# Two value projections as one Strassen product, the first heads' queries and keys as another, and the forget gates computed apart

## The chip, the cores and the metric

The kernel runs on one core of a Trainium2 chip, as one program. The metric is the device time of that core in microseconds (us); less is better. In the text PE is the matrix engine (TensorE), DVE the vector engine (VectorE), ACT the scalar engine (ScalarE), POOL GpSimd, SP the engine that issues the DMAs. PEld is the loading of a stationary operand (the weights of a matmul) into the matrix engine; it runs beside matmuls.

## The reference, cut to what matters

One layer of a hybrid encoder on x, 1024 tokens of 1024 channels, float32. All branches start from one projection of x; these are its parts that the change touches.

```python
proj = x @ w_in
q_a, k_a, v_a, f_a, q_b, f_b, i_b, g_b, gate_a, gate_b = jnp.split(proj, IN_SPLITS, axis=-1)
# widths: 512, 512, 512, 8, 512, 512, 512, 512, 1024, 1024
log_fa = jax.nn.log_sigmoid(f_a + b_f)                  # 8 heads
y_a = fox_attention(q_a, k_a, v_a, log_fa)              # logits: q.k/8 + F[t] - F[s], F = cumsum(log_fa)
o_b = hgrn2_chunkwise(silu(q_b), 1 - f, i_b, log(f))    # i_b: the values of the second branch
merged = sigmoid(gate_a) * (y_a @ w_pa) + sigmoid(gate_b) * (y_b @ w_pb)
x = layer_norm(ALPHA * x + merged @ w_o)
x = layer_norm(ALPHA * x + (silu(x @ w_g) * (x @ w_u)) @ w_ff_out)
```

The values of the first branch are `v_a` (512 columns), those of the second `i_b` (512 columns), and the forget gates `f_a` (8 columns).

## The kernel before, in words

**Precision.** Each float32 operand of a large product is split into a high part `hi` (rounded to the matmul type) and the rest `lo`; `split` (line 337) does it with one ACT copy and one DVE subtraction, and `mm3` (line 366) issues three matmuls, hi·hi, hi·lo and lo·hi, into one PSUM bank. Each matmul takes a 128x128 stationary block and at most 512 moving columns.

**Order of the work.** Nothing is issued when the code calls it. Every call goes into a list (`Plan.add`, line 90); `Plan.schedule` (line 161) then places the calls engine by engine, with a cost formula for each (`cost`, line 126), the order of the program as rank, and buffers handed out by tag; `issue` (line 269) emits them. So each engine has one fixed queue, and all instructions carry the line of the emitting call, L280. Calls made while `plan.early` is 3000 get a rank 3000 places earlier. In the formula a matmul of more than 128 columns costs `n / 2.4 + 13.4` ns and one of 128 or fewer 60 ns.

**The stages.**
1. Values of the first branch, `va` (from line 385): eight chunks of x and of the weights arrive by DMA, are split, and for each chunk the eight token blocks take three matmuls each, 192 of 128x512, into eight PSUM banks (`va_acc`). `X(c)` (line 374) gives the split chunks of x, which stay in `xh` and `xl` for later.
2. Values of the second branch and forget gates (lines 424 to 446): the 512 columns of `i_b` and the 8 of `f_a` lie side by side as 520 columns, cut into two halves of 260; eight token blocks times eight chunks times two halves times three give 384 matmuls of 128x260 (`vb_acc`). The values are copied out and stored to DRAM (`vb_d`), the gates go to `ft`.
3. Forget-gate chain (lines 448 to 474): eight transposes (`fps`) bring the gates to 8 partitions of 1024 tokens, and a chain of ACT and DVE operations on 8x1024 gives the log-sigmoid, its running sum, and its form for the reversed odd token blocks; it is stored to DRAM (`nf_d`).
4. `qk_project(0)` (line 479): queries and keys of heads 0 and 1, 96 matmuls of 128x512 (`qps`, `kps`).
5. `attention(p, qk)` for the four pairs of heads (line 501): for each head `nf_d` is broadcast to 128 partitions into `box1` (tag `m`), and eight blocks of 128 queries run through logits (`s`), softmax and the product with the values (`pt`, `pv`). Between the pairs come the projections of the next pair.
6. Four heads of the second branch (`hgrn_project`, `hgrn`), which read `vb_d`, and eight gate projections (`gate`, `gps`, `PLAIN = 8`). The gate projections stand last in the program but depend on nothing of the attention, so the schedule puts their matmuls wherever the attention and the second branch leave PE free.
7. The other eight gate projections (`GatePair`, `gs`) and the feed-forward layer (`Chunk`, `group`) are already Strassen products: seven products of half-size blocks in place of eight, with sums of blocks formed on DVE. Output projection and layer norms lie between.

`small` (line 315) hands out small per-partition columns with four buffers of each name; attention takes four of them per query block (`mx`, `nm`, `sm`, `rs`).

Of the kernel before, what the change touches and what calls it, by code (L numbers as in the profile page):

```python
# [27 lines left out]
WTAGS = ("qk",) * 6 + ("kb",) * 4 + ("pf",) * 4 + ("hl",) * 2  # L28
# [255 lines left out]
def trunk(ctx: ExitStack, tc, a: dict, out: bass.AP):  # L284
# [33 lines left out]
    def keep(shape, name, dt=F32):  # L318
        return plan.tile(cst, shape, dt, "k_" + name, name, 1)

    def const(name, shape, dt=F32):
        t = keep(shape, name, dt)
        sync.dma_start(t, a[name])
        return t
# [9 lines left out]
    def f(ap):  # L334
        return ap.bitcast(F32)
# [47 lines left out]

    idle = take("gt", [NB], "idle", BF16)
    dve.memset(idle, 0.0)
    stage = ["qk"] * 6 + ["kb"] * 2
    acc = [bank(ALL[t], f"va_acc{t}") for t in range(NT)]
    for _ in range(WARM):
        mm(acc[NT - 1], idle[:, :P], idle, start=True, stop=True)
    for c2 in range(KC // 2):  # L390
        raws = []
        wraw = take("pf", [2, NB], f"wva{c2}_r")
        for j in range(2):
            raw = full(stage[2 * c2 + j], f"x{2 * c2 + j}_r")
            parts = [slice(0, 256), slice(256, S)] if c2 + j == 0 else [slice(0, S)]
            for i, s_ in enumerate(parts):
                sync.dma_start(raw[:, s_], a["xT"][2 * c2 + j][:, s_])
                if c2 == 0 and i == 0:
                    sync.dma_start(wraw[:, j, :], a["w_va"][c2][:, j, :])
            if c2 and j == 0:  # L400
                sync.dma_start(wraw, a["w_va"][c2])
            raws.append((raw, parts))
        lane = lane_of(None)
        for j in range(2):
            c = 2 * c2 + j
            wh, wl = (take(f"w{n}{lane}", [NB], f"wva{c}_{n}", F32R) for n in "hl")
            h, l = X(c)
            raw, parts = raws[j]
            split(h[:, parts[0]], l[:, parts[0]], raw[:, parts[0]])
            split(wh, wl, wraw[:, j, :])  # L410
            for s_ in parts[1:]:
                split(h[:, s_], l[:, s_], raw[:, s_])
            for t in range(NT):
                mm3(acc[t], h[:, blk(t)], l[:, blk(t)], wh, wl, c == 0, c == KC - 1)
    va = take("v", [NT, NB], "va")
    for t in range(NT):
        (act.copy if t % 2 else dve.tensor_copy)(va[:, t, :], acc[t])

    ident = const("ident", [P, P])
    causal = const("causal", [P, 2, P], BF16)  # L420
    bf = const("bf", [HA, 1])


    box1 = take("m", [4, S], "box1")
    NV = NB + HA
    HV = NV // 2
    wv = []
    for c in range(KC):
        raw = raw_load(a["w_vb"][c], [NV], f"wvb{c}")
        hi, lo = (full(WTAGS[2 * c + j], f"wvb{c}_{'hl'[j]}", F32R)[:, :NV] for j in range(2))  # L430
        split(hi, lo, raw)
        wv.append((hi, lo))
    vb_d = dram.tile([NT, P, NB], F32, name="vb_d")
    ft = take("gt", [NT, HA], "ft")
    for t in range(NT):
# [7 lines left out]
        act.copy(vb[:, :HV], o[0])  # L443
        dve.tensor_copy(vb[:, HV:], o[1][:, :NB - HV])
        dve.tensor_copy(ft[:, t, :], o[1][:, NB - HV:])
        sync.dma_start(vb_d[t], vb)

    fz, fa, fe, fu = (full("pf", n)[:HA] for n in ("fz", "fa", "fe", "fu"))
    for hf in range(2):
        fps = bank("s", f"fps{hf}")  # L450
        for t in range(4):
            tr(fps[:HA, blk(t)], ft[:, 4 * hf + t, :], ident)
        dve.tensor_copy(fz[:, hs(hf)], fps[:HA])
    act.activation(fe, fz, AF.Abs, bias=bf, scale=1.0)
    dve.tensor_scalar(fa, fz, bf, 0.0, op0=ALU.add, op1=ALU.min)
    act.activation(fe, fe, AF.Exp, scale=-1.0)
    dve.tensor_scalar(fu, fe, 1.0, None, op0=ALU.add)
    act.activation(fz, fu, AF.Ln)
    dve.tensor_scalar(fu, fu, -1.0, None, op0=ALU.add)
    dve.tensor_sub(fe, fe, fu)  # L460
    act.activation(fu, fz, AF.Exp, scale=-1.0)
    dve.tensor_mul(fe, fe, fu)
    dve.tensor_add(fz, fz, fe)
    nf = box1[:HA, 2, :]
    dve.tensor_tensor_scan(nf, fz, fa, 0.0, op0=ALU.add, op1=ALU.subtract)

    nfv, fzv = (t.rearrange("p (j c t) -> p j c t", c=2, t=P) for t in (nf, fz))
    odd = fzv[:, :, 1, :]
    ends = [nfv[:, :, c, P - 1:P].to_broadcast([HA, 4, P]) for c in range(2)]
    dve.tensor_sub(odd[:, :, 1:], ends[1][:, :, 1:], nfv[:, :, 1, :P - 1])  # L470
    dve.tensor_sub(odd[:, :, 0:1], nfv[:, :, 1, P - 1:P], nfv[:, :, 0, P - 1:P])
    dve.tensor_add(nfv[:, :, 1, :], odd, ends[0])
    nf_d = dram.tile([HA, S], F32, name="nf_d")
    sync.dma_start(nf_d, nf)
# [3 lines left out]

    def qk_project(p):
        q2 = [full("qk", f"q2_{p}_{i}", F32R) for i in range(2)]  # L480
        k2 = [full("kb", f"k2_{p}_{i}", F32R) for i in range(2)]
        kl = [full("qk", f"kl_{p}_{i}", F32R) for i in range(2)]
        for b in range(2):
            w = weights(a["w_qk"][b, p], [KC, P], f"w{'qk'[b]}{p}", 0)
            for hf in range(2):
                o = bank("s" if p == 0 else "g", f"{'qk'[b]}ps{p}_{hf}")
                project(o, w, hf)
                for i in range(2):
                    me, ot = slice(i * DH, (i + 1) * DH), slice((1 - i) * DH, (2 - i) * DH)
                    if b == 0:  # L490
                        act.activation(q2[i][me, hs(hf)], o[me], AF.Copy, scale=0.125)
                        dve.scalar_tensor_tensor(q2[i][ot, hs(hf)], o[me], 0.125, f(q2[i])[me, hs(hf)],
                                                 op0=ALU.mult, op1=ALU.subtract)
                    else:
                        act.copy(k2[i][me, hs(hf)], o[me])
                        act.copy(k2[i][ot, hs(hf)], o[me])
                        dve.tensor_sub(kl[i][me, hs(hf)], o[me], f(k2[i])[me, hs(hf)])
                        act.copy(kl[i][ot, hs(hf)], f(kl[i])[me, hs(hf)])
        return q2, k2, kl

    def attention(p, qk):
        q2, k2, kl = qk
        for i in range(2):
# [4 lines left out]
            sync.dma_start(nfx[:, :, 1, :], nf_d[h].rearrange("(j t) -> j t", t=P).partition_broadcast(P))  # L508
# [9 lines left out]
            for qb in range(NT):  # L518
                n = (qb + 1) * P
                pt = full("pf", f"p{h}_{qb}") if qb > 3 else half("ph", f"p{h}_{qb}")  # L520
                mx = small([P, 3], "mx")
# [20 lines left out]
                nm = small([P, 1], "nm")  # L542
# [6 lines left out]
                sm = small([P, 1], "sm")  # L549
                act.activation(pt[:, :n], pt[:, :n], AF.Exp, bias=nm, scale=1.0, accum_out=sm)  # L550
                rs = small([P, 1], "rs")
# [30 lines left out]
    lmask = const("lmask", [P, 2, P], U16)  # L582
# [30 lines left out]
    def hgrn(h, qfg, box):  # L613
# [127 lines left out]
        for hf in range(2):  # L741
            op = bank("pv", f"op{h}_{hf}")
            ss = small([P, 4], "ss")
# [9 lines left out]
            rr = small([P, 4], "rr")  # L753
# [24 lines left out]
    qk = qk_project(0)  # L778
# [16 lines left out]

    def operand4(tags, name):
        ts = [[take(tags[2 * j + i], [2, NB], f"{name}{'hl'[i]}{j}", F32R) for j in range(2)] for i in range(2)]
        return [[ts[i][c // 2][:, c % 2, :] for c in range(4)] for i in range(2)]

    def operand1(tag, name):  # L800
        t = take(tag, [2, 4, NB], name, F32R)
        return [[t[:, i, c, :] for c in range(4)] for i in range(2)]

    def quarter(i, m):
        return [[x[i][:, c, hs(m)] for c in range(4)] for x in (xh, xl)]
# [54 lines left out]

    def sums4(op, dst, x, y, sub):
        for c in range(4):
            (dve.tensor_sub if sub else dve.tensor_add)(dst[c], x[c], y[c])
            split(op[0][c], op[1][c], dst[c])
# [124 lines left out]
    def layer_norm(t, gb, st=None, out=None):  # L989
        mv = small([P, 2], "mv")  # L990
        dve.bn_aggr(mv, (lnst[:, t] if st is None else st).rearrange("p a b -> p (a b)"))
        ve = small([P, 1], "ve")
        dve.tensor_scalar(ve, mv[:, 1:2], LN_EPS, None, op0=ALU.add)
        rstd = small([P, 1], "rstd")
# [368 lines left out]
def _constants():  # L1363
# [12 lines left out]
    return {"ident": ident, "causal": causal, "once": once,  # L1376
# [9 lines left out]
def _layout(x, w_in, b_fgate, hgrn_lb_logits, hgrn_norm_g, w_branch_a, w_branch_b, w_out, ln1_g, ln1_b,  # L1386
# [17 lines left out]
    def quarters(m):  # L1404
# [11 lines left out]
        "w_va": c(pairs(cols(2))[0]),  # L1416
        "w_vb": c(np.concatenate([cols(6), cols(3)], axis=1).reshape(KC, P, NB + HA)),
# [8 lines left out]
        "bf": c(np.asarray(b_fgate)[0].reshape(HA, 1)),  # L1426
# [22 lines left out]
```

## Time and profile before

| | |
|---|---|
| time, median of 3 runs | 1475.9 us (1475.35 to 1477.84) |
| the profiled execution | 1476.22 us |
| its span, first to last instruction | 1474.4 us |
| mean granted clock of PE | 0.998 |
| instructions | 19347 |
| HBM read, written | 134.52 MB, 39.09 MB |

A row of a group of instructions names the engine, the operation, the tiles written and read (`out<-in`), the shape and the count (`x96`), then the busy time and the mean ns of one. A row of the timeline starts with its start and its duration in us; `[0.78 <-ACT xh L280]` means that the engine stood idle 0.78 us before it, and for what. A row of the windows gives a stretch, its length, and for each engine the busy time and in brackets the number of instructions, then the granted clock, the share of the DMA engines and GB/s. Matmuls are pipelined: one of 512 columns shows a duration of 389 ns, though the next may start long before that is over, so the distance between starts tells the price of one, not the duration.

### The profile page before, as it was taken

To read this page: it belongs to the slowest core of one execution; us is meant where nothing else is said; L and a number is where in the kernel's file an instruction comes from. 1 tells how busy PE (TensorE), PEld (TensorE's weight loads), DVE (VectorE), ACT (ScalarE), POOL (GpSimd) and SP (SyncE) were. 2 spreads that over 40 slices of the span, in tenths; PEclk is the share of its full clock that TensorE was granted. 3 is DMA by queue.
4 is the path that set the end of the run, shared out by engine and by line. 5 is a ranking of instruction groups with operands and counts; after the bars stand their busy time and mean duration, and the time that the engine had idled before them with its cause. 6 is when DMAs were issued, how large, how long until landed. Compare 5 with 4: busy or idle time off the path is not lost.

```text
span 1474.4 us, 19347 instructions
## 1 busy us (share of the span) xinstructions
PE 1455.1 (99%) x7033; PEld 1208.2 (82%) x7033; DVE 1053.3 (71%) x1993; ACT 659.8 (45%) x1121; POOL 96.6 (7%) x116
## 2 busy tenths in 40 slices
PE   9999999999999999999999899999999999999998
PEld 7997888888887888788888788888888888888887
DVE  5237676686887899645848897676666666798597
ACT  5126667577568566234611443333333333534430
POOL 0004142130101000000001000000000000000000
PEclk9999999999999999999999999999999999999999
DMA  6202222121211235347610314232222335976741
GB/s 237 78 37 83 58 66 72 47 76 39 73 44 58 86 134 178 119 155 253 225 45 0 115 35 143 100 99 95 95 98 102 107 108 179 342 264 225 258 159 58
DMA packets 79566, 174.86 MB, mean 119 GB/s; under 512 B 7528, under 2 KB 20456, under 8 KB 79472
## 3 DMA queue, kind: packets, MB, share of 16 engines
q1 hardware_dynamic: 79472, 173.64, 34.9%
q8 instruction: 55, 0.90, 0.2%
q14 instruction: 39, 0.32, 0.1%
HBM read 134.52 MB, written 39.09 MB: 118 GB/s over the span
## 4 chain that ended last, share of the span: by engine, by line
PE 93%; DVE 4%; ACT 1%; DMA 1%; issue 0%; POOL 0%; SPq 0%; DVEq 0%; ACTq 0%; POOLq 0%
PE p L280 14%; PE fb L280 11%; PE fc L280 8%; PE fa L280 8%; PE bps L280 8%; PE pps L280 6%; PE o L280 6%; PE gs L280 5%; PE gps L280 5%; PE vb_acc L280 3%; PE va_acc L280 3%; PE kps L280 3%; PE pv L280 2%; PE s L280 2%; PE qps L280 2%; PE pt L280 2%
## 5 line engine op out<-in xcount | busy, mean ns | idle before, releaser
L280 PE MATMUL p<-dp 128*128 128x512 f32 (+1 forms) x957 | 210.0, 382 | 0.0
L280 PEld LDWEIGHTS p<-dp 128*128 128x128 f32 x957 | 175.3, 188 | 34.8
L280 PE MATMUL fc<-xs,Tp 128*128 128x512 f32 x528 | 127.0, 389 | 0.0
L280 PE MATMUL fb<-xs,Tp 128*128 128x512 f32 x528 | 126.7, 389 | 0.0
L280 PE MATMUL fa<-x,Tp 128*128 128x512 f32 x480 | 115.7, 389 | 0.3 <-DVE u L280 0.3
L280 PEld LDWEIGHTS fb<-xs,Tp 128*128 128x128 f32 x528 | 99.1, 188 | 20.6
L280 PEld LDWEIGHTS fc<-xs,Tp 128*128 128x128 f32 x528 | 99.0, 188 | 20.7 <-ACT xs L280 0.2
L280 ACT CAST Tp<-t 128x512 fp32r<-128x512 f32 x88 | 54.3, 620 | 116.2 <-PE fc L280 71.9
L280 PEld LDWEIGHTS fa<-x,Tp 128*128 128x128 f32 x480 | 90.0, 188 | 19.3 <-ACT p L280 0.7
L280 DVE TENSOR_TENSOR Tp<-t,Tp 128x512 fp32r<-128x512 f32 x88 | 60.6, 691 | 60.5 <-ACT Tp L280 60.0
L280 ACT CAST dp<-dap 128x1024 fp32r<-128x1024 f32 (+1 forms) x42 | 41.1, 982 | 99.3 <-PE p L280 45.3
L280 PE MATMUL bps<-xh,wb_l 128*128 128x512 f32 x192 | 76.0, 396 | 0.0
L280 PE MATMUL bps<-xh,wb_h 128*128 128x512 f32 x192 | 75.9, 395 | 0.0
L280 PE MATMUL bps<-xl,wb_h 128*128 128x512 f32 x192 | 75.9, 396 | 0.0
L280 POOL TENSOR_TENSOR rstd<-ve,mhalf 128x1 f32<-128x1 f32 x16 | 14.9, 932 | 887.4 <-DVE ve L280 887.4
L280 DVE TENSOR_TENSOR tl<-pt,th 128x512 fp32r<-128x512 f32 (+1 forms) x96 | 50.7, 552 | 20.3 <-ACT th L280 20.0
L280 DVE TENSOR_TENSOR dp<-dap,dp 128x1024 fp32r<-128x1024 f32 (+1 forms) x42 | 47.5, 1134 | 15.4 <-ACT dp L280 15.4
L280 PE MATMUL fb<-x,Tp 128*128 128x512 f32 x240 | 57.7, 389 | 0.0
L280 POOL TENSOR_SCALAR p<-p,rs 128x128 f32<-128x128 f32 (+3 forms) x64 | 47.5, 749 | 140.7 <-DVE rs L280 91.0
L280 ACT CAST th<-pt 128x512 fp32r<-128x512 f32 (+1 forms) x96 | 43.2, 479 | 28.3 <-PE pt L280 27.1
L280 ACT ACTIVATE p<-p,nm 128x128 f32<-128x128 f32 (+3 forms) x64 | 49.5, 776 | 9.0 <-DVE nm L280 8.5
L280 PEld LDWEIGHTS fb<-x,Tp 128*128 128x128 f32 x240 | 45.1, 188 | 9.4
(374 smaller groups left out, 3511.5 us busy)
## 6 DMA issues: line engine op xcount, KB each, us to landing
dbp<-in_w_fo SPq DMA_DIRECT2D x45, 512.0 KB, 4.8
dap<-a_d SPq DMA_DIRECT2D x35, 512.0 KB, 4.8
a_d<-ar SPq DMA_DIRECT2D x42, 256.0 KB, 3.7
wu_r<-in_w_ff SPq DMA_DIRECT2D x20, 512.0 KB, 3.6
wg_r<-in_w_ff SPq DMA_DIRECT2D x20, 512.0 KB, 3.6
a_d<-as SPq DMA_DIRECT2D x33, 256.0 KB, 2.4
wg_r<-in_w_g SPq DMA_DIRECT2D x16, 512.0 KB, 3.6
sg<-gate_d SPq DMA_DIRECT2D x32, 256.0 KB, 3.5
```

The costliest lines, as they stand in the source:

```text
L280: getattr(q.engine, method)(*args, **kw)
```

## The change

**One product for both values.** The weights of `v_a` and `i_b` stand side by side as a matrix of 1024 rows and 1024 columns, so that x times it is cut into halves each way: A11, A12 are the channel halves of the first 512 tokens, A21, A22 those of the last 512; B11, B21 belong to `v_a`, B12, B22 to `i_b`. Seven products p1 to p7 (four token blocks, four chunks, three matmuls each, 48 matmuls of 128x512) replace the two stages. DVE forms T1 = B12 - B11, T2 = B22 - T1, T4 = B21 - T2, T3 = T2 - B11, and of x S1 = A21 + A22, S3 = A11 - A21, S2 = A22 - S3, S4 = A12 - S2; every one of them is split before its product. The results are added on DVE into `va` and `vbm`, and `vbm` goes to `vb_d`. The input now comes in quarters of x (512 columns of tokens) and of the weights; B22 is loaded a second time for p3.

**First heads.** `qk_first` replaces `qk_project(0)`: the query weights and the key weights of heads 0 and 1 are the column halves, S1 to S4 are reused as moving operands, and seven products of 12 matmuls of 128x512 replace the 96. A21 is split a second time, since S1 had taken its place.

**Forget gates.** `forget_gates` is called in the middle of `qk_first`: for each of eight token blocks and eight chunks one matmul of x's hi part with the 16 columns hi and lo of the gate weights, and one of x's lo part with the 8 columns hi: 128 matmuls (`fo`) of 16 or 8 moving columns, each with its own 128x128 stationary block of x. One transpose brings them to 64 partitions (token block times head) of 128 tokens; the chain runs on 64x128, and a matmul with a constant matrix (`before`) and three DVE operations replace the long running sum and the reversal.

**Rest.** `small` columns of one use are merged into one tile (`soft`, `norm`, `ss`); `causal` and `lmask` share a buffer; `box1` is taken after `vbm` (both have tag `m`). On the queues of the built program PE has 4163 entries where there were 4287, DVE 2032.

```diff
-    acc = [bank(ALL[t], f"va_acc{t}") for t in range(NT)]
...
-            for t in range(NT):
-                mm3(acc[t], h[:, blk(t)], l[:, blk(t)], wh, wl, c == 0, c == KC - 1)
...
-    for t in range(NT):
-        vb = half(("tt", "ph")[t % 2], f"vb{t}")
-        o = [bank(("pt", "h")[t % 2], f"vb_acc{t}_{i}")[:, :HV] for i in range(2)]
-        for i in range(2):
-            r = slice(i * HV, (i + 1) * HV)
-            for c in range(KC):
-                h, l = X(c)
-                mm3(o[i], h[:, blk(t)], l[:, blk(t)], wv[c][0][:, r], wv[c][1][:, r], c == 0, c == KC - 1)
...
+    A11, A12, A21, A22 = quarter(0, 0), quarter(1, 0), quarter(0, 1), quarter(1, 1)
+    vops = {"p1": A11, "p2": A12, "p4": A22}
+    vx, vy = ([bank(ALL[4 * i + t], f"v{'xy'[i]}{t}") for t in range(4)] for i in range(2))
...
+    def v_mul(p, T, o, first, outer=False):
+        more = {} if first else {"skip_group_check": True}
+        A = vops[p]
+        for t, c in ((t, c) for t in range(4) for c in range(4)) if not outer else ((t, c) for c in range(4) for t in range(4)):
+            mm3(o[t], A[0][c][:, blk(t)], A[1][c][:, blk(t)], T[0][c], T[1][c], first and c == 0, c == 3, more)
...
+    T1, T2, T4, T3 = rows(b12), rows(b22), rows(b21), rows(b11)
+    for dst, x, y in ((T1, T1, T3), (T2, T2, T1), (T4, T4, T2)):
+        for c in range(4):
+            dve.tensor_sub(dst[c], x[c], y[c])
+    split4(A22, a22)
...
+    product("p4", T4, vx, True)
+    for t in range(4):
+        dve.tensor_add(va[:, t, :], vy[t], p1v[t])
+    for t in range(4):
+        act.copy(va[:, 4 + t, :], vx[t])
+    vops["p5"] = A21
+    for c in range(4):
+        s1 = half("gt", f"vs1r{c}")
+        dve.tensor_add(s1, a21[c], a22[c])
+        split(vops["p5"][0][c], vops["p5"][1][c], s1)
+    product("p5", T1, vy, True)
...
+    for c in range(4):
+        s3 = half("gt", f"vs3r{c}")
+        dve.tensor_sub(s3, f(A11[0][c]), a21[c])
+        dve.tensor_add(s3, s3, f(A11[1][c]))
+        dve.tensor_sub(a22[c], a22[c], s3)
+        split(vops["p6"][0][c], vops["p6"][1][c], a22[c])
+        split(vops["p7"][0][c], vops["p7"][1][c], s3)
+    product("p6", T2, vx, True)
...
+    product("p7", T3, vx, False)
...
+    product("p3", rows(b22), vy, False)
+    for t in range(4):
+        dve.tensor_add(p1v[t], vx[t], p1v[t])
+        dve.tensor_add(va[:, 4 + t, :], va[:, 4 + t, :], p1v[t])
+        dve.tensor_add(vbm[:, 4 + t, :], vbm[:, 4 + t, :], p1v[t])
...
+    def forget_gates():
+        split(wf[:, :, :HA], wf[:, :, HA:], wfr)
+        fo = bank("h", "fo")[:, :2 * NT * HA].rearrange("p (t h) -> p t h", h=2 * HA)
+        for t in range(NT):
             for c in range(KC):
                 h, l = X(c)
+                mm(fo[:, t], h[:, blk(t)], wf[:, c], start=c == 0, stop=c == KC - 1)
+                mm(fo[:, t, :HA], l[:, blk(t)], wf[:, c, :HA], start=False, stop=c == KC - 1, skip_group_check=True)
+        ft = half("gt", "ft")[:, :NT * HA].rearrange("p (t h) -> p t h", h=HA)
+        act.copy(ft, fo[:, :, HA:])
+        dve.tensor_add(ft, fo[:, :, :HA], ft)
+        BH = NT * HA
+        fps = bank("h", "fps")[:BH, :P]
+        tr(fps, ft.rearrange("p t h -> p (t h)"), ident)
...
+        base = bank("h", "fbase")[:BH, :1]
+        mm(base, before[:, :BH], nf[:, P - 1:P], start=True, stop=True)
...
+    def qk_first():
...
+        mul("p5", b12, oc, True)
+        act.copy(p5, oc)
+        split4(A21, a21)
+        mul("p1", b11, oa, True)
+        act.copy(p1, oa)
+        mul("p2", b21, oa, False)
+        dve.tensor_sub(t2, b22, b12)
+        forget_gates()
+        qk_heads(0, 0, oa, *tiles)
+        mul("p6", t2, ob, True)
+        dve.tensor_add(u2, ob, p1)
+        mul("p3", b22, oc, False)
+        dve.tensor_add(u2, oc, u2)
+        qk_heads(1, 0, u2, *tiles)
...
-    qk = qk_project(0)
+    qk = qk_first()
+    box1 = take("m", [4, S], "box1")
```

More of the change, by code (lines that the diff above doesn't have):

```diff
@@ L433, in trunk, with block @@
[L433 to L439 removed]
+        mm(vy[3], idle[:, :P], idle, start=True, stop=True)
+    def block(k, n, tags, name):
+        return [take(tag, [2, NB], f"{name}_{i}", F32) for i, tag in enumerate(tags)], a["w_v"][k, n]
@@ new lines, in load, with rows, stationary4 @@
+    def load(b, cs=range(4)):
+        tiles, src = b
+        for c in cs:
+            sync.dma_start(tiles[c // 2][:, c % 2, :], src[c])
+    def rows(b):
+        return [b[0][c // 2][:, c % 2, :] for c in range(4)]
+    xa = take("m", [KC, NB], "xa_r")
+    b11 = block(0, 0, ("kb", "kb"), "b11")
+    b21 = block(1, 0, ("pf", "pf"), "b21")
+    ring = [0]
+    def stationary4(name):
+        n = ring[0]
+        ring[0] ^= 1
+        tags = (("wh0", "wh0", "wh1", "wh1"), ("wl0", "wl0", "wl1", "wl1")) if not n else (("ph",) * 4, ("tt",) * 4)
+        return [[half(tags[i][c], f"T{name}{'hl'[i]}{c}", F32R) for c in range(4)] for i in range(2)]
@@ new lines, in trunk @@
+    b12 = block(0, 1, ("qk", "qk"), "b12")
+    b22 = block(1, 1, ("qk", "qk"), "b22")
+    load(b12)
+    load(b22)
+    ax = take("x", [2, 4, NB], "x2_r")
+    a21, a22 = ([ax[:, i, c, :] for c in range(4)] for i in range(2))
+    for c in range(4):
+        sync.dma_start(a22[c], a["xT"][4 + c][:, hs(1)])
+    for c in range(4):
+        sync.dma_start(a21[c], a["xT"][c][:, hs(1)])
+    p1v = [take("kb", [2, NB], f"p1v{i}") for i in range(2)]
+    p1v = [p1v[t // 2][:, t % 2, :] for t in range(4)]
@@ new lines, in trunk, with product @@
+    va = take("v", [NT, NB], "va")
+    for t in range(4):
+        act.copy(p1v[t], vx[t])
+    T1, T2, T4, T3 = rows(b12), rows(b22), rows(b21), rows(b11)
+    for dst, x, y in ((T1, T1, T3), (T2, T2, T1), (T4, T4, T2)):
+        for c in range(4):
+            dve.tensor_sub(dst[c], x[c], y[c])
+    split4(A22, a22)
+    def product(p, src, o, first):
+        T = stationary4("v" + p)
+        split4(T, src)
+        v_mul(p, T, o, first)
+    product("p4", T4, vx, True)
+    for t in range(4):
+        dve.tensor_add(va[:, t, :], vy[t], p1v[t])
@@ new lines, in trunk @@
+    ident = const("ident", [P, P])
+    causal = const("causal", [P, 2, P], BF16, "mask")
+    bf = const("bf", [NT * HA, 1])
+    before = const("before", [NT * HA, NT * HA + 2])
+    vops["p3"] = operand4(("kb", "kb", "qk", "qk"), "vs4")
+    for c in range(4):
+        dve.tensor_sub(a22[c], f(A12[0][c]), a22[c])
+        dve.tensor_add(a22[c], a22[c], f(A12[1][c]))
+        split(vops["p3"][0][c], vops["p3"][1][c], a22[c])
+    b22 = block(1, 1, ("hl", "hl"), "b22_2")
+    load(b22)
+    product("p3", rows(b22), vy, False)
@@ L445, in trunk @@
[L445 to L468, printed above, removed]
@@ new lines, in forget_gates @@
+                mm(fo[:, t, :HA], l[:, blk(t)], wf[:, c, :HA], start=False, stop=c == KC - 1, skip_group_check=True)
[5 more added lines that the diff above has]
+        tr(fps, ft.rearrange("p t h -> p (t h)"), ident)
+        f4 = half("gt", "f4")[:BH]
+        fz, fa, fe, fu = (f4[:, blk(i)] for i in range(4))
+        act.activation(fe, fps, AF.Abs, bias=bf, scale=1.0)
@@ L485, in qk_project @@
             for hf in range(2):
-                o = bank("s" if p == 0 else "g", f"{'qk'[b]}ps{p}_{hf}")
+                o = bank("g", f"{'qk'[b]}ps{p}_{hf}")
                 project(o, w, hf)
[L488 to L498, printed above, removed]
```

195 lines of the change are left out of this document (120 added, 75 removed).

## The prediction

> **What bounds the kernel now.** I read the page first: busy time and the chain that ended last.
>
> ```profile
> PE 1455.1 (99%) x7033; PEld 1208.2 (82%) x7033; DVE 1053.3 (71%) x1993; ACT 659.8 (45%) x1121; POOL 96.6 (7%) x116
> PE 93%; DVE 4%; ACT 1%; DMA 1%; issue 0%; POOL 0%; SPq 0%; DVEq 0%; ACTq 0%; POOLq 0%
> ```
>
> PE is the bound, all through. So a change is worth the PE time that it removes, less the waits that it puts in front of PE. The change touches the stretch up to the first logits. The windows show what the others do there:
>
> ```profile
> core 0: us, PE busy (x) PEld busy (x) DVE busy (x) ACT busy (x) POOL busy (x), PEclk, DMA share, GB/s
> 0.00:10.00 10.00, 8.00 (x25) 4.09 (x26) 3.72 (x7) 5.21 (x7) 0.20 (x4) 1.00 0.81 282
> 10.00:20.00 10.00, 10.00 (x46) 8.29 (x45) 8.86 (x10) 7.21 (x10) 0.00 (x0) 1.00 1.03 403
> 0.00:120.00 120.00, 116.43 (x688) 100.97 (x689) 47.72 (x78) 40.66 (x63) 0.20 (x4) 1.00 0.33 115
> ```
>
> DVE is busy 47.72 of 120 us: there is room. The DMA engines are full up to 20 us.
>
> After that stretch PE stays covered. The gate projections fill its gaps, and some are left when the second branch is done:
>
> ```profile
> L280 PE MATMUL op<-box,qeb x56: 275/275/275, 392.5 to 563.8; 128*128 128x128 f32 x56
> L280 PE MATMUL gps<-xh,wg_l x128: 387/393/480, 120.8 to 571.0; 128*128 128x512 f32 x128
> ```
>
> The filler ends at 571.0, the branch at 563.8. In the order of the changed program 37 gate matmuls stand behind the last `op`, where 29 did, and from the Strassen gates (`gs`) on the two orders are nearly the same. So what PE gains or loses before the first logits comes through to the end; I cost everything after that at nothing. Without filler up to there, a later attention would show up instead.
>
> **The prices.** For a matmul I take the distance between starts.
>
> ```profile
> 8.13 41.78 PE va_acc L280 x183
> 49.91 45.55 PE vb_acc L280 x384
> 96.86 0.39 PE L280 MATMUL qps<-xh,wq_h 128*128 128x512 f32 x1
> 106.83 0.39 PE L280 MATMUL qps<-xh,wq_l 128*128 128x512 f32 x1
> ```
>
> The first two rows are pieces of the chain of waits: 384 matmuls of 260 columns in 45.55 us, 0.1186 each. The last two are the first and last of 45 in the timeline: 9.97/44 = 0.2266 us for 512 columns. (The 183 of `va_acc` give 0.2283, with small waits.)
>
> The forget gates' 128 matmuls have 16 or 8 columns, but each loads a new 128x128 stationary block. No row has such a pair. The nearest are the first logits, 128 columns wide, and the loads around them:
>
> ```profile
> 120.10 0.22 PE L280 MATMUL s<-k,q 128*128 128x128 f32 x1
> 120.16 0.28 PE L280 MATMUL s<-kl,q 128*128 128x128 f32 x1
> 120.27 0.45 PE L280 MATMUL gps<-xh,wg_h 128*128 128x512 f32 x1
> ...
> 120.11 0.19 PEld L280 LDWEIGHTS s<-kl,q 128*128 128x128 f32 x1
> 120.21 0.19 PEld L280 LDWEIGHTS gps<-xh,wg_h 128*128 128x128 f32 x1
> 120.33 0.19 PEld L280 LDWEIGHTS gps<-xl,wg_h 128*128 128x128 f32 x1
> ```
>
> A matmul can follow in 0.06 us when its weights are there, but the next then starts 0.11 later, since loads follow each other at 0.10 to 0.12. I take one load per matmul, 0.11: 128 x 0.11 = 14.1 us. The lower bound is 0.06 each, 7.7 us; the upper is load and matmul one after the other, 0.17 each, 21.8 us.
>
> [...]
>
> **The sum on PE.**
> - Both values: before 192 x 0.2266 + 384 x 0.1186 = 43.5 + 45.5 = 89.0; after 7 x 48 = 336 x 0.2266 = 76.1. Gain 12.9.
> - First queries and keys: 96 matmuls become 84. Gain 12 x 0.2266 = 2.7.
> - The eight gate transposes go, a transpose and a small matmul come.
>
> ```profile
> 95.28 0.93 PE L280 MATMUL fps<-ident,ft 128*8 128x128 f32 x7
> ```
>
> Seven take 0.93 us with the drain of the last (0.27), so about 0.11 each: 0.9 goes, 0.2 comes. Gain 0.7.
> - Forget gates apart: loss 14.1. In before they rode as 8 of 520 columns, almost free.
>
> PE work: 12.9 + 2.7 + 0.7 - 14.1 = 2.2 us less. The large gain of the product is nearly eaten by the small matmuls.
>
> **The waits before.** From the first useful matmul to the first logits:
>
> ```profile
> 4.43 0.76 PE L280 MATMUL va_acc<-wva_h,xh 128*128 128x512 f32 x2
> 5.96 0.40 PE L280 MATMUL va_acc<-wva_h,xl 128*128 128x512 f32 x1
> 7.14 0.50 PE L280 MATMUL va_acc<-wva_h,xh 128*128 128x512 f32 x1 [0.78 <-ACT xh L280]
> PE kps L280 <- DVE wk_l L280: 1.6, 2, 1.3
> ```
>
> 120.10 - 4.43 = 115.7 us, work 89.0 + 0.9 + 21.8 = 111.7: 4.0 us of waits, some 1.7 at the start (x's first chunk comes whole) and the rest in `kps`, whose splits queue on DVE behind the gate chain.
>
> **The waits after.** DVE gets much more. In the product stage I count, in DVE's order, 120 operations of 512 columns: 56 low-part subtractions of splits and 64 sums or result additions. Their pace, back to back:
>
> ```profile
> 96.53 0.67 DVE L280 TENSOR_TENSOR vhl<-va,vhl 128x512 fp32r<-128x512 f32 x1
> 97.13 0.67 DVE L280 COPY fz<-fps 8x512 f32<-8x512 f32 x1
> 97.73 0.67 DVE L280 TENSOR_TENSOR vhl<-va,vhl 128x512 fp32r<-128x512 f32 x1
> ```
>
> 0.60 each, so 72 us beside 76.1 of PE. It fits, narrowly; ACT has 69 copies at about 0.6, 41 us. Walking through DVE's queue against PE's, with DMA landings estimated from the rates of the windows:
> - Start: the first chunk is 512 columns, not 1024, so PE waits less: 1.0 in place of 1.7.
> - p4 starts near 27 us. [...] T1 can start with B12, about 17; T1, T2, T4, T4's splits and one addition are 17 operations, 10.4 us, so A22's first low part comes near 28.5, where p4's fourth matmul asks for it at 27.9. Wait 0.6.
> - p6 starts near 49.5. DVE has 24 operations between p5's last split (about 39.9) and p6's last weights, 14.5 us; the PE order takes 16 matmuls (3.6 us) of the ready chunks first. Wait 0.7.
> - SP issues the input in 45 pieces before A21 is complete, at the pace of this row, 15 us, ahead of the landings: nothing.
>
> ```profile
> 95.97 0.32 SPq L280 DMA_DIRECT2D vb_d<-vb  x1
> ```
>
> - p5, p7, p3 find their operands; result additions wait for single banks and are not behind PE.
> - `qk_first`: p2's bank waits for ACT's copy of p1 behind splits, 0.3. The gate chain is off PE's path: 128 columns in place of 1024, some 4 us, and 17 matmuls (3.9 us) stand between its transpose and its small matmul; 0.3.
> - First logits: the keys' sum needs p3, then ACT and DVE five operations of about 0.6, behind two splits queued first; 13 matmuls (2.9 us) of cover. Wait 0.7.
>
> Together 3.6 us, 0.4 less than before. Where the old chain goes, the attention's `box1` is no longer late: the key heads are late next, as just priced. `qk_first` leaves 12 matmuls for after the first logits; they count in the sum. The merged `soft` columns keep one buffer per block from maximum to POOL's scaling; four blocks stay in flight, the gates fill PE: nothing.
>
> Gain 2.2 + 0.4 = 2.6 us. The profiled execution took 1476.22, 1.8 more than its span and 0.3 more than the median 1475.9. From the median: 1473.3.
>
> **The rivals.**
>
> 1. **Forecast: the small matmuls eat the gain** (0.55). 1473.3, own range 1470.5 to 1476: the listed waits may be 0 or double.
>
> 2. **The clock falls in the gate stretch** (0.18; slower). What idleness does stands in the trace once, in the feed-forward's first wait:
>
> ```profile
> 834.02 1.22 PE L280 MATMUL fa<-x,Tp_0h 128*128 128x512 f32 x2 [4.14 <-ACT Tp_0h L280]
> 834.75 0.29 PEld L280 LDWEIGHTS fa<-x,Tp_0l 128*128 128x128 f32 x1 [0.23 <-DVE Tp_0l L280]
> 833.00:834.00 1.00, 0.00 (x0) 0.00 (x0) 0.08 (x1) 0.65 (x2) 0.00 (x0) 0.98 1.05 430
> 834.00:835.00 1.00, 0.98 (x2) 0.75 (x3) 1.00 (x2) 1.00 (x3) 0.00 (x0) 0.50 1.01 414
> 837.00:838.00 1.00, 1.00 (x5) 0.78 (x5) 1.00 (x3) 0.06 (x1) 0.00 (x0) 0.82 0.32 123
> ```
>
> After 4.14 us without matmuls the clock was 0.50 from 834.0 to about 837.4, and a load grew from 0.19 to 0.29. In the gate stretch 112 matmuls in a row, 12.3 us, stream 8 or 16 columns per 0.11 us, under a tenth of the time that 512 columns stream. [...] Against it: loads run all the time, and loads may count. [...]
>
> 3. **DVE becomes the bound of the product stage** (0.12; slower). A low-part subtraction shows 0.69 us by itself:
>
> ```profile
> L280 DVE TENSOR_TENSOR wva_l<-wva_r,wva_h 128x512 fp32r<-128x512 f32 x8 | 5.4, 688 | 3.0 <-ACT wva_h L280 3.0
> ```
>
> If waits on ACT keep the 120 from overlapping, they take 82.6 us, 10.6 over; PE's lead at p4, p6 and the keys absorbs about 3. 1473.3 + 7 = 1480.
>
> 4. **Load and matmul in a row**, 0.17 each (0.07; slower): 1473.3 + 7.7 = 1481.
>
> 5. **Small matmuls at 0.06** (0.08): 1473.3 - 6.4 = 1467.
>
> **How the numbers follow.** 0.2% is about what a measurement of this kernel can tell from no change; it is 2.95 us, so faster is below 1472.95, slower above 1478.85. The forecast lies close to that border: of its 0.55 I give 0.27 to faster, 0.26 to within, 0.02 to slower; rival 5 gives 0.08 to faster; of 2, 3 and 4 (0.37) 0.05 falls within. Faster 0.35, same 0.31, slower 0.34. The range 1467.5 to 1482.5 leaves out about half of rival 5 and of rival 2's upper end, and little of 3 and 4.
>
> **What would show it.** Right: loads of `fo` 0.11 apart, granted clock 1.00 throughout, first logits near 115 us, p4 and p6 with waits under 1 us each. Rival 2: clock 0.50 about 95 to 108 us. Rival 3: PE waits on DVE at p4, p5, p6 in several places, first logits after 120. Wrong altogether: a time away from the sum while the first logits come at 115; then the cause lies in the attention's new order.

## The result and the profile after

The changed kernel took 1493.17 us (median of 4 runs, 1492.29 to 1495.01), the kernel before beside it 1476.54 us (4 runs): ratio 1.0114, 95% interval 1.0097 to 1.0132. It is 1.1% slower. The forecast was 1473.3 us and the range ended at 1482.5. The profiled execution after took 1494.05 us with a span of 1492.3, before 1474.4: 17.9 us to be found.

First the page of the kernel after: busy times, the granted clock in 40 slices, and the shares of the chain that ended last.

```profile
PE 1466.3 (98%) x6904; PEld 1212.6 (81%) x6904; DVE 1106.9 (74%) x2085; ACT 676.9 (45%) x1162; POOL 96.6 (6%) x116
...
PEclk9978999999999999999999999999999999999999
...
PE 86%; DVE 6%; DMA 4%; ACT 1%; issue 1%; POOL 1%; SPq 0%; DVEq 0%; ACTq 0%; POOLq 0%
```

PE is busy 11 us longer although the trace has 129 of its matmuls fewer (6904 for 7033, and on DVE 2085 operations for 1993; the counts under "The change", 4163, 4287 and 2032, are not those of the profiles), and the third and fourth slices (75 to 149 us) have a 7 and an 8 in the clock's line, where the kernel before has a 9 in every slice. So one looks there. The chain of waits up to the end of that stretch (start, length, what; `x48` is the number of instructions):

```profile
28.81 11.70 PE vx L279 x48
40.51 10.88 PE vy L279 x48
51.39 21.94 PE vx L279 x96
73.33 10.88 PE vy L279 x48
84.21 5.44 PE qk_s L279 x24
89.65 1.68 PE fo L279 x16
91.33 2.88 PE qk_s L279 x12
94.22 21.37 PE fo L279 x112
115.59 1.91 PE qk_pt L279 x4
...
117.71 3.21 PE qk_pt L279 x8
...
126.23 12.52 DMA box<-nf_d
```

The product stage is as forecast: the 48 matmuls of p5 and the 48 of p3 take 10.88 us each time, 0.2267 a matmul, and the values are done at 84.21, where they were done at 95.46 before. Then the gates: the first 16 at 0.105 each, the other 112 at 0.191. The last row is a surprise of another kind: 12.5 us for a broadcast. The timeline shows the change of pace (start, duration):

```profile
96.43 0.26 PE L279 MATMUL fo<-wf,xh 128*128 128x16 f32 x1
96.54 0.27 PE L279 MATMUL fo<-wf,xl 128*128 128x8 f32 x1
96.67 0.36 PE L279 MATMUL fo<-wf,xh 128*128 128x16 f32 x1
96.89 0.35 PE L279 MATMUL fo<-wf,xl 128*128 128x8 f32 x1
```

0.11 us from start to start up to 96.54, about 0.21 behind it. Read in windows of 0.2 us, the clock of this trace goes between 1.00 and 0.50 at 96.64, 120.53, 137.60, 141.01, 850.98, 854.40 and 1489.28 us and nowhere else; the distances are 7, 5, 1, 208, 1 and 186 times 3.413 us. In the 3.413 us before the first fall PE streams columns for about a third of the time; in the 3.413 us before those, after which the clock stays at 1.00, for about 58%. (Estimates from the starts in the timeline: 0.95 and 1.93 us of the wide `qk_s`, and 22 and 12 gate matmuls at 0.2267 us for 512 columns.) The windows of the same kernel, all engines (busy time and instructions of PE, PEld, DVE, ACT, POOL, then the granted clock):

```profile
90.00:100.00 10.00, 10.00 (x64) 9.47 (x64) 6.35 (x10) 4.25 (x8) 0.00 (x0) 0.83 0.00 1
100.00:110.00 10.00, 10.00 (x49) 10.00 (x48) 0.00 (x0) 0.00 (x0) 0.00 (x0) 0.50 0.01 2
110.00:120.00 10.00, 10.00 (x38) 8.95 (x38) 1.28 (x5) 1.48 (x5) 0.00 (x0) 0.50 0.06 8
130.00:140.00 10.00, 6.19 (x24) 4.79 (x23) 4.96 (x18) 5.92 (x13) 3.46 (x3) 0.88 0.39 82
140.00:150.00 10.00, 9.41 (x48) 7.47 (x48) 8.68 (x35) 4.97 (x12) 5.46 (x8) 0.95 0.33 107
```

Full PE and a full load queue, and half the clock. And 130 to 140 us has a hole in PE, 6.19 of 10. What it is, from the timelines of PE, DVE and POOL, and the landing times of the broadcast (before, then after; the last number is the median us from issue to landing):

```profile
136.65 0.44 PE L279 MATMUL s<-k,q 128*128 128x384 f32 x1 [3.81 <-DVE soft L279]
...
136.30 0.29 DVE L279 CUSTOM_DVE_ANT_0 p<-s,box 128x128 f32<-128x128 f32 x1 [4.08 <-POOL box L279]
...
135.11 2.27 POOL L279 TENSOR_TENSOR box<-box,causal 128x512 f32<-128x512 f32 x2 [134.67 <-ACT wq_h L279]
```
```profile
box<-nf_d SPq DMA_DIRECT2D x8, 512.0 KB, 4.2
```
```profile
box<-nf_d SPq DMA_DIRECT2D x8, 512.0 KB, 8.9
```

PE waits for the softmax, the softmax on DVE for the box, the box on POOL for the DMA that spreads a head's gates over 128 partitions (the page puts POOL's wait down to an ACT copy that had long been done; the chain above has the DMA). That DMA moves the same 512 KB as before in twice the time. The change stores the box as [token block, head, 128], so a head's values are eight pieces of 512 B, 4096 B apart, where they were one piece of 4 KB. This edit was in the diff; the prediction did not price it.

### The profile page after: what moved, and what is told of

Read it like the earlier page. It is cut to its first block, busy times and chain, and to the rows that moved or that the text cites. A ratio compares the mean times of both kernels' runs of the same rounds, so it can differ in the third digit from the quotient of the medians.

```text
span 1492.3 us, 19241 instructions
## 1 busy us (share of the span) xinstructions
PE 1466.3 (98%) x6904; PEld 1212.6 (81%) x6904; DVE 1106.9 (74%) x2085; ACT 676.9 (45%) x1162; POOL 96.6 (6%) x116
## 4 chain that ended last, share of the span: by engine, by line
PE 86%; DVE 6%; DMA 4%; ACT 1%; issue 1%; POOL 1%; SPq 0%; DVEq 0%; ACTq 0%; POOLq 0%
PE p L279 14%; PE fb L279 11%; PE fc L279 8%; PE fa L279 8%; PE bps L279 7%; PE pps L279 6%; PE o L279 6%; PE gs L279 5%; PE gps L279 3%; PE vx L279 2%; PE pv L279 2%; PE kps L279 2%; PE pt L279 2%; PE qps L279 2%; PE fo L279 2%; PE vy L279 1%
## 5 line engine op out<-in xcount | busy, mean ns | idle before, releaser
L279 PE MATMUL fa<-x,Tp 128*128 128x512 f32 x480 | 115.7, 389 | 0.3 <-DVE u L279 0.3
L279 POOL TENSOR_TENSOR norm<-norm,mhalf 128x1 f32<-128x1 f32 x16 | 14.6, 913 | 890.2 <-DVE norm L279 890.2
L279 ACT ACTIVATE p<-p,soft 128x128 f32<-128x128 f32 (+3 forms) x64 | 49.6, 776 | 19.0 <-DVE soft L279 18.6
L279 POOL TENSOR_SCALAR p<-p,soft 128x128 f32<-128x128 f32 (+3 forms) x64 | 49.0, 773 | 113.9 <-DVE soft L279 106.4
```

Source lines behind the costliest of these rows:

```text
L279: getattr(q.engine, method)(*args, **kw)
```

## The experiments

Two theories, each with a rival. **A:** matmuls of 8 or 16 columns behind a load of 0.11 us stream too little for the clock to stay, so it halves in the gate stretch; rival: the fall has another cause, and wider matmuls at the same pace would not hold it up. **C:** the box is late because of how it lies in DRAM; rival: it is late only because the gates are. Behind both stands the question whether the rest of the change brings what the prediction summed. Where no interval is given, a time is of one run, and runs of one kernel lie up to 5.5 us apart (run 9: 1474.64 to 1480.18), so differences of 2 us between such times say little; the kernel before took 1477.71 us beside the first four, 1476.6 (19 runs) beside the next four, 1477.01 (18 runs) beside the last three.

**1. 128 columns per gate matmul.** The same 128 loads; each matmul streams 128 columns in place of 16 or 8. Those beside the gates' columns are junk, and the results are spread over more banks.

```diff
...
-                mm(fo[:, t], h[:, blk(t)], wf[:, c], start=c == 0, stop=c == KC - 1)
-                mm(fo[:, t, :HA], l[:, blk(t)], wf[:, c, :HA], start=False, stop=c == KC - 1, skip_group_check=True)
+                fo, u, r = fos[t // per], t % per, wfx[:, 2 * HA * c:2 * HA * c + FW]   # FW = 128
+                mm(fo[:, u], h[:, blk(t)], r, start=c == 0, stop=False)
+                mm(fo[:, u], l[:, blk(t)], r, start=False, stop=c == KC - 1)
...
```

> The changed kernel, but each of the 128 gate matmuls streams 128 columns (16 of the gate weights, the rest junk that nobody reads) in place of 16 or 8. Loads, their number and order stay. Theory A (the clock falls because few columns stream; a window of 3.4 us with a third of it streamed already counted as idle, one with 55% did not): 128 columns are 53 of each 112 ns, so the granted clock stays 1.00 over the gates, their long stretch takes 12.5 us in place of 21.4, and the following matmuls lose nothing: about 11 us less, 1482, with the later wait for the bias broadcast still there. Theory B (load after load is what counts as idle, whatever streams): clock 0.50 and 1493 as before.

Measured: 1482.68 us, 10.5 less than the change, for eight times the columns and more. Its windows:

```profile
90.00:100.00 10.00, 10.00 (x80) 9.51 (x79) 6.67 (x11) 4.69 (x9) 0.00 (x0) 1.00 0.00 1
100.00:110.00 10.00, 10.00 (x78) 9.36 (x77) 1.46 (x7) 1.24 (x5) 0.00 (x0) 1.00 0.06 12
```

78 matmuls between 100 and 110 us where the change had 49, at a clock of 1.00. A holds, its rival falls.

**2. 32 columns.** The same edit with `FW = 32`.

> The same with 32 columns, 13 of each 112 ns. Theory A with a border between a third and a half of a window: the clock falls as with 16, 1493. If the border lies below 12% and only the 3 to 6% of the change were too little: clock 1.00, 1482.

Measured: 1495.84 us, the clock falls as in the change. The two windows around the fall (PE's busy time, matmuls, granted clock):

```profile
96.00:98.00 2.00, 2.00 (x18) 0.84 0.02 4
98.00:100.00 2.00, 2.00 (x11) 0.50 0.00 0
```

**3. The box stored by head.** The rows of the 64-partition chain are ordered head, then token block, and so is the tensor; the gates stay thin.

```diff
-    nf_d = dram.tile([NT, HA, P], F32, name="nf_d")
+    nf_d = dram.tile([HA, NT, P], F32, name="nf_d")
...
-            sync.dma_start(nfx[:, :, 1, :], nf_d[:, h, :].partition_broadcast(P))
+            sync.dma_start(nfx[:, :, 1, :], nf_d[h].partition_broadcast(P))
```

> The changed kernel, with the gate results stored by head (partition = head times 8 + block, so a head's 1024 values lie together in DRAM, as they did before the change) in place of by block. Theory C (the broadcast of a head's bias to 128 partitions is slow because its eight pieces of 512 bytes lie 4 KB apart): it lands in 4 to 5 us as before the change, not 9 to 12.5; the matrix engine's wait of 3.8 us at the first logits and the fall of the clock behind it go, 5 to 6 us less, 1488. Rival D (it is slow because of the fewer bytes per packet or of other transfers at that time): still 9 us or more, 1493.

Measured: 1489.04 us, 4.1 less than the change. The median landing and PE's wait for the softmax:

```profile
box<-nf_d SPq DMA_DIRECT2D x8, 512.0 KB, 4.2
```
```profile
PE s L279 <- DVE soft L279: 1.7, 2, 0.9
```

The gates are nearly as late as in the change (the last of them ends 1.1 us earlier), the wait is 1.7 us instead of 3.8, and the clock does not fall a second time; so the layout makes the box late, and C holds. Not all that this run saved is the layout's. Its gates in the chain:

```profile
95.00 19.45 PE fo L279 x112
```

The same thin matmuls took 1.9 us less than in the change, because the clock fell later, at 99.5 us, and stayed at half for 20.5 us where it was 23.9. The span is 5.1 us shorter than in the change: 2.4 less of waits for the softmax (`soft` and `p`) and 1.7 without the second fall are the box's, 4.1 together, and about 1.1 come from the later fall in the gates.

**4. Operands exchanged, old chain.** PE holds the 40 gate-weight columns (8 high, 24 zeros, 8 low) and x streams: 32 matmuls of 512 columns for the 128 thin ones. The gates come out on 8 partitions and go through the chain of the kernel before.

```diff
...
+        for hf in range(2):
...
+            for c in range(KC):
+                mm(fo, wf[:, c], h[:, hs(hf)], start=c == 0, stop=False)
+                mm(fo, wf[:, c], l[:, hs(hf)], start=False, stop=c == KC - 1)
...
```

> The gates computed with exchanged operands: the gate weights (40 columns with zeros between hi and lo) are the stationary block and x streams, 32 matmuls of 512 columns in place of 128 thin ones; the gate chain is again the one on 8 partitions of 1024, and stored by head. Theory A: clock 1.00; 32 x 0.227 = 7.3 us of matmuls in place of 23.1 measured, 2.4 back behind them, 5.5 back at the first logits, so about 1470. If what the product stage itself lost is more than I think (its waits on the vector engine, the long chain on 8 partitions holding up the first softmax), 1475 or more.

Measured: 1475.11 us, clock 1.00 through the gates. Better than the kernel before beside it by 2.6 us, but of one run, and 5 us above what was expected: new waits stand in the product stage (1.6 us on `vs4h`) and in the attention's start (1.0 on `wg_h`). The zero filling takes a buffer that the product stage uses; run 9, which does without it, has no wait on `vs4h`.

**5. Both repairs.** Edits 1 and 3 together.

> The changed kernel with both repairs at once: each gate matmul streams 128 columns (16 or 8 of them used, the others junk), and the box is stored by head, so that a head's values lie in one piece. If the clock's fall in the gates (theory A: 1493.2 to about 1482.7, 10.5 us) and the box's broadcast in eight pieces (theory C: 1493.2 to about 1489.0, 4.1 us) are two causes that add up, 1493.2 - 10.5 - 4.1 = 1478.6, with the clock at 1.00 from 90 to 125 us and the median landing of nf_d near 4.2 us. Then the parts of the change outside the gates and the box are worth nothing, or 1 to 2 us of loss. If a third cause of the loss remains, 1481 or more; if the change's other parts do bring what the prediction summed, 1475 or less.

Measured: 1479.73 us (10 runs, 1478.06 to 1482.11), ratio to before 1.0020, interval 1.0011 to 1.0030. The two causes add up (10.5 + 4.1 = 14.6, measured 13.4), and what remains is a loss of 3 us where the prediction had a gain of 2.6. In its chain the gates and p6 of the first heads cost what they should at full clock (the profiled execution took 1478.06 us, and its span is 1.9 us above that of before):

```profile
94.20 12.45 PE fo L279 x112
106.65 0.98 PE qk_pt L279 x4
...
107.74 1.86 PE qk_pt L279 x8
```

Against the change that is 8.9 us less for the 112 and 2.3 less for the 12 of p6, which still lay in the half-clock stretch. The loss that remains is in the waits behind the first logits. Before, then this run, from 118 us to the feed-forward:

```profile
PE ot L280 <- DVE ob L280: 1.6, 1, 1.6
PE ot L280 <- DVE tot L280: 0.7, 1, 0.7
```
```profile
PE ot L279 <- DVE ob L279: 2.2, 2, 1.5
PE op L279 <- DVE ob L279: 1.2, 1, 1.2
PE op L279 <- DVE at L279: 1.0, 2, 0.6
PE pt L279 <- DVE tl L279: 0.8, 1, 0.8
PE s L279 <- DVE soft L279: 0.5, 2, 0.3
```

With two of 0.4 and 0.3 more (`qps` and `pt`) that is 6.4 us against 2.3; the waits of `gs` are the same in both and left out. All of it lies in the two attention branches, whose order on the queues the change has altered. That the new order makes these waits was not tried by itself. Where PE stands at two points: at the second matmul of the first logits (in before at 120.16, shown above; here from the timeline), and at the last gate projection (before, then here; first and last start stand behind the durations):

```profile
119.50 0.39 PE L279 MATMUL s<-kl,q 128*128 128x128 f32 x2
```
```profile
L280 PE MATMUL gps<-xh,wg_h x128: 387/393/481, 120.3 to 570.6; 128*128 128x512 f32 x128
```
```profile
L279 PE MATMUL gps<-xh,wg_h x128: 387/393/481, 123.0 to 572.7; 128*128 128x512 f32 x128
```

At the first point it is 0.7 us ahead, with four matmuls of the next heads (0.9 us) already done: 1.6 ahead. At the second it is 2.1 behind. 1.6 - 4.1 = -2.5: the waits account for it within half a microsecond.

**6. Operands exchanged, chain of the change.** As 4, with eight small transposes to 64 partitions and the box by head.

> The changed kernel with the gates' operands exchanged: the weights' 40 columns (8 high, 24 zeros, 8 low) are held in PE and x streams, 32 matmuls of 512 columns and 8 small transposes for the 128 thin matmuls; then the chain on 64 partitions as the change has it, box stored by head. 32 x 0.2266 + 8 x 0.11 = 8.1 us for the gates against 14.3 with one load each at full clock: about 6 us below the run with 128 columns and the box by head (expected 1478.6), so 1472.5, and faster than the kernel before (1476.5). Clock 1.00 through 90 to 125 us. If the longer chain (two sums, eight transposes and a copy behind the last gate matmul) makes the box late, a wait of the first softmax for the box appears and 1475 to 1478 results, no better than the variant with the chain on 8 partitions (1475.1).

Measured: 1478.57 us (10 runs, 1476.69 to 1479.97), ratio 1.0011, interval 1.0002 to 1.0021. The gates and their transposes cost some 6 us less, and most of it came back: the values are done at 87.17 us where run 5 has 84.23, behind the wait on `vs4h` below, and the wait for the softmax is 2.0 us where run 5 has 0.5.

```profile
PE s L279 <- DVE soft L279: 2.0, 1, 2.0
PE vy L279 <- ACT vs4h L279: 1.6, 1, 1.6
```

**7 and 8. Distance of the pieces.** Both have 128 columns, pieces of 512 B and eight stores in place of one (so that the tensor may have gaps); in 7 an unused row follows each eight heads, so that the pieces are 4608 B apart, in 8 they stay 4096 B apart. If the distance makes the broadcast slow, it is fast in 7 alone; if eight pieces in place of one do, whatever their distance, it is slow in both.

```diff
-    nf_d = dram.tile([NT, HA, P], F32, name="nf_d")
+    nf_d = dram.tile([NT, HA + 1, P], F32, name="nf_d")     # 7 only
...
+        for t in range(NT):
+            sync.dma_start(nf_d[t, :HA], nf[t * HA:(t + 1) * HA])
```

> 128 columns for each gate matmul (junk beside the 16 or 8 used), and the box in DRAM with one unused row of 128 values behind each eight heads, so that the eight pieces of a head's values lie 4608 B apart in place of 4096; written by eight DMAs in place of one. [...]

> Control for the run with the padded box: the same kernel with the eight writing DMAs and 128 columns, and the pieces 4096 B apart as in the change. Landing of nf_d's median near 8.8 us and about 1482.7 by both theories; if it lands in about 4.2 us, the eight writes and not the distance made the difference in the other run.

Measured: 1480.19 us padded, 1485.38 unpadded, one run each. Nothing but the distance differs between the two, so the 5.2 us are put down to it. Run 7 lies 0.5 us above run 5, which has one piece, and run 8 2.7 above what was expected of it; with eight stores 4.7 us pass from the first store's issue to the first broadcast's, where run 5 with one has 1.8. The profile gives no landing for these broadcasts; their issue on SP and the time when POOL could begin stand for it, padded and then unpadded:

```profile
117.94 1.02 SPq L279 DMA_DIRECT2D box<-nf_d  x2
122.50 5.42 POOL L279 TENSOR_TENSOR box<-box,causal 128x512 f32<-128x512 f32 x4 [122.06 <-DMA box<-nf_d]
```
```profile
117.34 1.02 SPq L279 DMA_DIRECT2D box<-nf_d  x2
126.19 2.27 POOL L279 TENSOR_TENSOR box<-box,causal 128x512 f32<-128x512 f32 x2 [125.75 <-DMA box<-nf_d]
```

4.6 against 8.9 us (run 5, one piece, has 4.2 by the same measure). So eight pieces 4608 B apart took 0.4 us more than one piece, and eight pieces 4096 B apart 4.7 us more. Why that distance is slow is not shown.

**9 and 10. Sixteen columns held, and the gates one product earlier.** 9 holds the change's own 16 columns (8 high, 8 low) and adds the two halves after the transposes, so nothing is filled with zeros. 10 is the same with one call moved:

```diff
         act.copy(p1, oa)
+        forget_gates()
         mul("p2", b21, oa, False)
         dve.tensor_sub(t2, b22, b12)
-        forget_gates()
```

> As the run with 40 held columns and the chain on 64 partitions, but the gate weights are the 16 columns of the change (8 high, 8 low), no zeros are written, and high and low sums are added after the eight small transposes: 32 matmuls of 512 columns, box by head. It takes away the wait that the zero filling put in the product stage (1.6 us on vs4h in that run). Against the run with 128 columns and the box by head (1479.7) the gates take 32 x 0.2266 + 8 x 0.11 = 8.1 us in place of 14.4. If PE's order alone decides: 1479.7 - 6.3 = 1473.4. If the box is now the later one, as the 2.0 us wait of the logits' tile for the softmax in that run suggests (box's first sum at 119.0 there, PE at the softmax about 116 here), most of that comes back as a wait of s for soft of 2 to 4 us: about 1476.5. Clock 1.00 up to 140 us by both.

> The same with the gates called one product earlier (before p2 of the first heads, 12 matmuls = 2.7 us sooner on PE). If the box was the later one, it now comes about 2.7 us earlier and the wait of s for soft shrinks to about 1 us or less: 2 to 2.5 us faster than the kernel without this move, about 1474. If PE's order decides, no difference between the two.

Measured: 9 took 1477.79 us (10 runs; ratio 1.0006, 0.9996 to 1.0015), 10 took **1472.77 us** (9 runs, 1471.90 to 1475.35; ratio 0.9974, 0.9964 to 0.9984). So 10 beats the kernel before by 0.26% and the change by 1.4%. For 9 that is close to the second of its two expectations. The move was worth 5.0 us where 2 to 2.5 were expected, and the reason given for it was only half right. PE's wait for the softmax is 3.0 us in 9 and 1.1 in 10. DVE's timeline shows what the softmax stood behind in 9, and where it begins in 10:

```profile
115.88 2.90 DVE L279 TENSOR_TENSOR wg_l<-wg_r,wg_h 128x512 fp32r<-128x512 f32 x2 [0.84 <-ACT wg_h L279]
118.82 3.09 DVE L279 SCALAR_TENSOR_TENSOR q<-qk_p,q 64x512 fp32r<-64x512 f32 x2
121.94 0.29 DVE L279 CUSTOM_DVE_ANT_0 p<-s,box 128x128 f32<-128x128 f32 x1
```
```profile
116.65 0.29 DVE L279 CUSTOM_DVE_ANT_0 p<-s,box 128x128 f32<-128x128 f32 x1
```

In 9 two splits of gate weights and two operations that form the queries, 6 us together, stand ahead of the first softmax operation in DVE's fixed queue; with the gates earlier, the schedule puts the softmax first. The box itself is only 1.7 us earlier (POOL begins at 113.78 in place of 115.51). In 9 the clock also falls once more behind the wait of 3.0, with 1.6 on `wg_h` shortly before it (0.83 on average over 120 to 130 us).

**11. 96 columns.** As 1 with 96.

> The changed kernel with 96 columns for each gate matmul (16 or 8 used, the others junk): load-bound at 0.112 us each, a stream of 96 columns takes 0.2266 x 96/512 = 0.042 us of it, 38%. With 32 columns (13%) the clock fell as in the change, with 128 (51%) it did not. If the border lies under 38%, the clock stays at 1.00 through the gates and the time is about 1482.7, as with 128; if above, the clock falls for some 20 us and the time is about 1494.

Measured: 1491.46 us; the clock falls, about 3.4 us later than in the change:

```profile
98.00:100.00 2.00, 2.00 (x20) 1.00 0.00 0
100.00:102.00 2.00, 2.00 (x12) 0.51 0.04 8
```

With 38% of the time streamed the clock falls (one run), with 51% (128 columns, runs 1, 5, 7 and 8) it stays; both shares are estimates from 0.2266 us for 512 columns and 0.112 for a load. That the fall comes later is no evidence by itself: in run 3, with the thin matmuls of the change, it came 2.9 us later too. It fits if the stretches of 3.413 us lie as in the change, for the one before 96.6 also holds a microsecond of the wide `qk_s` matmuls; that they lie so here is not shown.

## Why the prediction was wrong, point by point

- **The price of a gate matmul: right, at full clock.** The forecast had 0.11 each, one load; the trace has 0.105 to 0.112, and the 112 take 12.45 us in run 5. Rivals 4 and 5 (0.17 and 0.06) fall.
- **The clock: the step that failed first.** The sum has the gates as 128 x 0.11 = 14.1 us, which holds only at full clock; they took 1.68 + 21.37 = 23.1. Rival 2, "The clock falls in the gate stretch", had a chance of 0.18; it came true. When the clock would fall and for how long, on which the upper end of the range rested, was the author's estimate; no row of before shows it. The runs showed 11.2 us in the chain (8.9 in the gates, 2.3 in p6): the fall came 2.4 us into the stretch, so some 90 of the 112 lay in it, and the clock stayed at 0.50 for 23.9 us, to 120.5 (it averaged 0.66 over 96 to 98 us and 0.87 over 120 to 122). When in the stretch it falls is not fixed: in run 3, with the same matmuls, it was 4.5 us in. "Against it: loads run all the time, and loads may count" weighed too much: PEld was busy 10.00 of 10 us at a clock of 0.50. No row of before has such thin matmuls back to back, so its trace could not decide it; run 1 and run 2 do.
- **"I cost everything after that at nothing": the second step that failed,** twice. "The attention's `box1` is no longer late" took the chain's shorter arithmetic for the box's arrival and left the broadcast out: 4.2 us became 8.9, PE waited 3.8 and the clock was at 0.50 once more, from 137.60 to 141.01 us (about 1.7 us lost). Run 3 gives 4.1 us for it. And behind the first logits the two attention branches have 4.1 us more waits (run 5), although the gate projections lasted as long as the prediction said they would. The filler stood behind the waiting matmul in PE's fixed queue and did not cover its wait: in the change PE was idle 3.81 us before the `s` of 136.65, with the gate projections behind it from 137.58 on.
- **The sums of the products and the waits up to the first logits: about right.** 79.7 us for the value products (4.55 to 84.21) against 76.1 of work, so 3.6 of waits where 2.3 were forecast. p4's was 0.7 (0.6 forecast), though for A22's high part from ACT and not for its low part from DVE; p6 had none (0.7 forecast); the start took 1.8 (1.0 forecast), and p4's own matmuls 0.8 more than their pace. Rival 3 falls: DVE is busy 40.00 of 40 us between 40 and 80, as narrow as forecast, and PE too. "First logits near 115 us": run 5 has the first of them at 115.7, but its partner with the low part stands behind the 12 matmuls of p4 and starts at 119.5; only then is PE comparable. Two sums of the prediction do not come out, and neither touches the miss: waits of 0 or double would give 1469.7 to 1476.9 and not 1470.5 to 1476, and the 10.6 us of rival 3 are counted over DVE's own 72 where PE's 76.1 is the mark (6.5).
- **The sum.** 11.2 (clock in the gates) + 5.0 (box: 3.3 more wait than in run 5, and 1.7 of clock) + 1.9 (run 5's span over that of before) = 18.1, measured 17.9.

## What to carry to other kernels

Price a matmul with a thin moving side by its load (0.105 to 0.112 us here), but first ask how much of the time PE really streams (here the clock fell to 0.50 at an estimated 38%, 96 columns, and stayed at 1.00 at 51%, 128 columns, while PE was busy 10.00 of 10 us in both), and where that is too little, exchange the operands, so that the thin matrix is held and the wide one streams (32 matmuls in 7.4 us in run 9 for 128 in 23.1). When a tensor's layout in DRAM changes, price every DMA that reads it (here 4.2 us became 8.9), and when a long stage gets shorter, look at what the next in-order queue puts ahead of the operation that now comes due.

## What the runs showed of the hardware

- Matmuls back to back that stream 8 to 96 columns behind a load of 0.112 us let the granted clock fall to 0.50 (the change, runs 2, 3 and 11); with 128 columns it stayed at 1.00 through the gates (runs 1, 5, 7 and 8).
- At a granted clock of 0.50 the gate matmuls of the change, one load each, started about 0.21 us apart, at 1.00 0.11.
- The clock stayed at 0.50 for 23.9 us in the change, 20.5 in run 3, 17.1 in run 11, and 3.4 in before (834.0 to 837.4) and in the change's second and third fall: seven, six and five times 3.413 us, and one.
- From the issue of a broadcast of 4 KB to 128 partitions to the start of its reader 4.2 us passed with one piece (run 5), 4.6 with eight pieces 4608 B apart (run 7) and 8.9 with eight pieces 4096 B apart (run 8).
- Some DVE operations beside POOL's box sums were slow: in run 9 two `wg_l` took 2.90 us and two `q` 3.09 while POOL was busy from 115.5 to 121.4, where one takes 0.6 to 0.7 elsewhere. Not all were: in run 10 the first softmax operation took 0.29 us beside POOL as it did in run 9 after it. The cause was not tried.
